# A quarter of the weight split moved from DVE to an accumulating DMA, in a four-mixer encoder layer

## The chip, the cores and the metric

The kernel runs on one core of a Trainium2 chip. The metric is the device time of one execution in microseconds (us). The engines are named as in the profile: PE is TensorE's matmul stream and PEld its weight loads, DVE is VectorE, ACT is ScalarE, POOL is GpSimd, and SP is SyncE, which here only issues DMAs.

## The reference, cut to what matters

One layer of an encoder trunk on 256 tokens of width 2048, all in float32: a norm, a mixer of three kinds of heads, a cross-attention to a memory of 256 tokens, and a convolutional FFN of width 5632. Nearly all of the work is in the products with the seven weight matrices, each used once:

```python
x = _layer_norm(x, ln_in_g, ln_in_b)
for l in range(DEPTH):                       # DEPTH = 1
    mix = _hybrid_mixer(x, w_in[l], ..., w_out[l])
    x = _layer_norm(DN_ALPHA * x + mix, ln1_g[l], ln1_b[l])
    ca = _memory_cross_attention(x, mem, xq[l], xkv[l], xo[l])
    x = _layer_norm(DN_ALPHA * x + ca, ln2_g[l], ln2_b[l])
    ff = _conv_ffn(x, ffn_w_up[l], ffn_conv_w[l], ffn_conv_b[l], ffn_w_down[l])
    x = _layer_norm(DN_ALPHA * x + ff, ln3_g[l], ln3_b[l])
```

## The kernel before

A float32 product is made of three products of the format f32r: each operand is written as a high part plus a low part, and high x high, high x low and low x high are summed in PSUM.

**The weight stream.** The weights lie in HBM in the order of their use and come in tiles of up to 1 MB (128 partitions x 2048 numbers), issued by SP into `wraw`, a pool of three buffers (line 110). `load_w` takes each tile in two halves of up to 128 x 1024. For each half, `split` makes the high part with a cast on ACT (line 142, `hi<-raw`) and the low part with a subtraction on DVE (line 143, `lo<-raw,hi`), into the pool `whl`, which has four buffers for `hi` and four for `lo`. So the split of a half can begin when PE has finished the half four before it, and PE then works on the three halves in between. A `raw` buffer is free for the next load when both its halves are split.

**The products.** `cm_chunk` (lines 155 and 157) computes 256 output channels with the channels on the partitions, `tm_part` (line 178) a token-major product; both walk over the halves in order and after each one call `tick`, which lets the running jobs (attention heads, convolution, norms) put their next few instructions in between.

**The norms.** After each of the first three norms `ln_affine` multiplies the stream `xt` by the norm's gain and adds its bias on POOL, off the main path. It works in four chunks. Each one loads two rows (`gb`, line 264, one buffer), multiplies two tiles (line 275) and adds to two tiles (line 276).

**Order.** Each engine runs its instructions in one fixed order, which a scheduler makes from the program when the kernel is built. An instruction that waits holds up everything behind it on its engine. A DMA is issued from an engine's own queue: when it has to wait for its data, that engine waits.

Of the kernel before, what the change touches and what calls it, by code (L numbers as in the profile page):

```python
# [7 lines left out]
F32 = mybir.dt.float32  # L8
F32R = mybir.dt.float32r
AF = mybir.ActivationFunctionType  # L10
ALU = mybir.AluOpType
AX = mybir.AxisListType

P = 128
D = 2048
S = 256
KT = D // P          # 16 contraction tiles of the model width
NT = S // P          # 2 token tiles
HM = 4               # mLSTM heads
HA = 8               # chunked-attention heads  # L20
HX = 4               # cross-attention heads
DFF = 5632
FT = DFF // P        # 44
CT = 31              # conformer taps
# [3 lines left out]
THREE = ((0, 0), (0, 1), (1, 0))     # the products of high and low parts that float32 sees  # L28
WT = 2048            # elements per partition of one streamed weight tile
WH = WT // 2         # elements per partition of one split weight tile  # L30
COLS = [(0, 512), (512, 1024), (1024, 1536), (1536, 2048)]
COLS_LAST = COLS[:3] + [(1536, 1792), (1792, 2048)]     # before a norm that nothing covers: a short last product
# [3 lines left out]
# per-partition parameter columns  # L36
# [10 lines left out]
def tm_group(n):  # L47
    """contraction tiles in one streamed tile of n token-major columns"""
    return 4 if n > 256 else 8
# [3 lines left out]
def trunk_kernel(ctx: ExitStack, tc: tile.TileContext, plan, x, memT, wts, pvec, rows, gbias, abias, normg, out):  # L53
    nc = tc.nc
    V, A, G = nc.vector, nc.scalar, nc.gpsimd
# [11 lines left out]
    # ---------------------------------------------------------------- constants  # L67
# [12 lines left out]
    def keep_warm(n):  # L80
        """products nobody reads: they hold the tensor engine's clock up where it waits for data"""
        ps = aux.tile([P, 512], F32, name="aux")
        for _ in range(n):
            last = nc.tensor.matmul(ps[:, 0:P], lhsT=ident, rhs=ident, start=True, stop=True)
        return tc.issue_after(last.ins)

    # ---------------------------------------------------------------- weight stream
    woff = [0]
    ready = []
    behind = []  # L90

    def fetch_w(mat, ks, cols):
        """next streamed weight tile: contraction tiles ks of the column ranges; plan records it for the host's layout"""
        n = sum(b - a for a, b in cols)
        sz = len(ks) * n
        raw = wraw.tile([P, WT], F32, name="raw")[:, :sz]
        src = wts[woff[0]:woff[0] + P * sz].rearrange("(p f) -> p f", p=P)
        woff[0] += P * sz
        plan.append((mat, tuple(ks), tuple(cols)))
        return raw, src  # L100

    def load_w(mat, ks, cols):
        """a streamed weight tile in halves, each split into two f32r parts: (contraction tiles, high, low)"""
        hk = step = (len(ks) + 1) // 2
        if ready:
            raw = ready.pop()
            step = 1 if ks[0] == 0 else hk
        else:
            raw, src = fetch_w(mat, ks, cols)
            nc.sync.dma_start(raw, src)  # L110
        n = raw.shape[1] // len(ks)
        for k0 in range(0, len(ks), hk):
            kl = ks[k0:k0 + hk]
            sz = len(kl) * n
            hi = whl.tile([P, WH], F32R, name="hi")[:, :sz]
            lo = whl.tile([P, WH], F32R, name="lo")[:, :sz]
            after = behind.pop(0) if behind else None
            for o in range(0, sz, step * n):
                e = min(o + step * n, sz)
                with tc.issue_after(after) if after else ExitStack():  # L120
                    split(hi[:, o:e], lo[:, o:e], raw[:, k0 * n + o:k0 * n + e])
            yield kl, hi.rearrange("p (k n) -> p k n", n=n), lo.rearrange("p (k n) -> p k n", n=n)

    # work that is spread between the weight tiles: every tick takes each running job one step on
# [11 lines left out]
    def split_to(dst, src):  # L136
        """the two parts of channel tiles [128, tiles, 256] into dst [128, tiles, 2, 256]"""
        split(dst[:, :, 0, :], dst[:, :, 1, :], src)

    def split(hi, lo, src):  # L140
        """src (f32, SBUF or PSUM) = hi + lo, each a f32r number"""
        A.copy(hi, src)  # L142
        V.tensor_sub(lo, src, hi.bitcast(F32))  # L143

    def cm_chunk(a, mat, c0, c1, dst):
        """256 channel-major outputs, 128 from column c0 and 128 from c1: dst[c, j, t] = sum_k W[k, cj + c] a[k, t]

        The two parts of a lie side by side, so that one product takes both of them."""
        ps = mm.tile([P, 2, 2, S], F32, name="mm")
        for g in range(0, KT, 8):  # L150
            for ks, wH, wL in load_w(mat, list(range(g, g + 8)), [(c0, c0 + P), (c1, c1 + P)]):
                for j in range(2):
                    cs = slice(j * P, (j + 1) * P)
                    for kk, k in enumerate(ks):
                        nc.tensor.matmul(ps[:, j], lhsT=wH[:, kk, cs], rhs=a[:, k], start=(k == 0), stop=(k == KT - 1),  # L155
                                         skip_group_check=True)
                        nc.tensor.matmul(ps[:, j, 0, :], lhsT=wL[:, kk, cs], rhs=a[:, k, 0, :], start=False,  # L157
                                         stop=(k == KT - 1), skip_group_check=True)
                tick()
        A.copy(dst, ps[:, :, 1, :])  # L160
        V.tensor_add(dst, dst, ps[:, :, 0, :])
# [5 lines left out]
    def tm_part(ps, a, mat, ks, cols, first=True, last=True, row0=0):  # L167
        """token-major outputs: psum[tt][t, c] += sum_k a[k, t] W[k, c] over the contraction tiles ks"""
# [13 lines left out]
    def tm_by_token(a, mat, ks, cols, row0=0):  # L182
        """as tm_part, one token tile after the other, so that the first one's norm runs under the second one's products"""
# [17 lines left out]
    def act_parts():  # L201
        """both parts of a channel-major operand: [channel, contraction tile, part, token]"""
        return act.tile([P, KT, 2, S], F32R, name="parts")

    # ---------------------------------------------------------------- layer norm
    xt = const.tile([P, NT, D], F32, name="xt")      # residual / pre-norm / normalised stream, in place

    def rsqrt(y, v, n):
        """y = 1/sqrt(v + eps): square root, reciprocal and a Newton step on [128, n]"""
# [10 lines left out]
    def ln_scales(n, tts=range(NT), last=None):  # L220
        """mean and 1 / std of token tiles from n partial statistics"""
# [7 lines left out]
    def ln_normalise(mv, rs, c, tts=range(NT)):  # L229
        """xt <- (xt - mean) / std on a quarter of the channels"""  # L230
# [5 lines left out]
    def ln_transpose(a, gname, bname, k0, nk=2):  # L236
        """channel-major g * z + b of nk channel tiles, split in two parts"""
# [24 lines left out]
    def pool_load(dst, src):  # L262
        """a small load behind what the Pool engine has to do before, off the weights' queue"""
        tc.keep_in_program_order(G.dma_start(dst, src))

    def ln_affine(ri, rs):
        """xt <- g * xt + b along the free dimension, chunk by chunk"""
# [10 lines left out]
    # ---------------------------------------------------------------- start: one head of the memory, input norm  # L278
# [6 lines left out]
    def load_both(mp, g, mat, cols):  # L285
        """a quarter of the memory and its weight tile, in halves that arrive by turns"""
# [48 lines left out]
    # ================================================================ mixer  # L335
    mix = act_parts()
    with tc.tile_pool(name="mx", bufs=1) as mx, tc.tile_pool(name="mx2", bufs=2) as mx2:
        # masks
# [13 lines left out]
        # ---- token-major slices of the projection  # L352
# [5 lines left out]
        # slice 0: gates and the first three value heads  # L358
# [8 lines left out]
        def gate_job():  # L367
            # log sigmoid(f) = min(f, 0) - log1p(e),  e = exp(-|f|),  log1p(e) = e ln(u) / (u - 1),  u = 1 + e
# [17 lines left out]
            # gates as rows: [head, time]  # L386
# [6 lines left out]
            # b = cumsum(log f); a = i - b; mrow = running max of max(a, 0); -m_t = -(b + mrow)  # L393
# [28 lines left out]
        # ---- conformer convolution channels  # L422
# [24 lines left out]
        # layer norm over the 512 channels (partitions x 4): sums by the tensor engine  # L447
# [41 lines left out]
        # ---- chunked attention heads  # L489
# [44 lines left out]
        # ---- mLSTM heads  # L534
# [5 lines left out]
        def mlstm_job(h, qp):  # L540
# [7 lines left out]
            # decay weights exp(a_s - mrow_t), keys on the partitions  # L548
# [29 lines left out]
        # normaliser max(|den|, exp(-m_t)), head norm and output gate  # L578
# [44 lines left out]
        # ---- output projection: the mLSTM channels come last  # L623
# [6 lines left out]
    # ---------------------------------------------------------------- residual + statistics of a token-major product  # L630
# [22 lines left out]
    # ================================================================ memory cross-attention  # L653
# [94 lines left out]
    # ================================================================ convolutional FFN  # L748
# [30 lines left out]
    # ---------------------------------------------------------------- output norm  # L779
# [73 lines left out]
```

## Time and profile before

| | |
|---|---|
| three runs | 1549.06, 1550.57, 1554.81 us; median 1550.57 |
| span of the profiled execution | 1549.5 us, first to last instruction |
| PE, DVE, ACT, POOL busy | 1522.2, 1022.2, 758.8, 141.3 us |
| DMA | 292.87 MB, of which the weights' queue 282.64 MB |
| weight halves on PE | 536 splits, each a cast on ACT and a subtraction on DVE |

The page gives the profiled execution by its span only, which lies 1.1 us under the median of the three runs. Busy shares are of the span. A wait counts only where the engine that waits is the one whose end sets the time.

### The profile page before, as it was taken

What the parts mean: (1) busy time and instruction counts of PE and PEld (TensorE: products, weight loads), DVE (VectorE), ACT (ScalarE), POOL (GpSimd) and SP (SyncE); (2) the same over time, 40 slices, a digit from 0 to 9 for tenths busy, and PEclk for the clock granted to TensorE, in tenths of its full rate; (3) what the DMA queues carried; (4) which work ended last, traced back from release to release, by engine and by line L of the source; (5) the groups of instructions that cost most, each with busy time, mean ns of one, the idle gap of its engine ahead of it and who ended that gap; (6) DMA issues with size and microseconds to landing.
All of it is one profiled execution on the core that took longest, in us unless ns stands there. A gap on an engine that the chain in (4) does not pass through costs nothing.

```text
span 1549.5 us, 20637 instructions
## 1 busy us (share of the span) xinstructions
PE 1522.2 (98%) x8218; PEld 1314.6 (85%) x8218; DVE 1022.2 (66%) x1346; ACT 758.8 (49%) x986; POOL 141.3 (9%) x138
## 2 busy tenths in 40 slices
PE   8999999999999999999989999999999999999995
PEld 7988888888888888888878888888888888888885
DVE  6765999678776545665579665566656665556666
ACT  5554454676454445454355554454534554455542
POOL 0350000100006300000036000000000000000002
PEclk9999999999999999999999999999999999999998
DMA  9565545444656654444555555545555554655452
GB/s 344 177 231 191 190 173 179 168 170 160 236 202 216 218 192 170 157 140 159 192 202 204 202 187 183 199 183 188 177 204 190 191 191 170 209 192 184 175 177 90
DMA packets 46127, 292.87 MB, mean 189 GB/s; under 512 B 5392, under 2 KB 6032, under 8 KB 15312
## 3 DMA queue, kind: packets, MB, share of 16 engines
q1 hardware_dynamic: 43056, 282.64, 50.3%
q0 software_dynamic: 2544, 8.13, 2.3%
q8 instruction: 64, 1.05, 0.3%
q10 hardware_dynamic: 432, 0.79, 0.1%
q14 instruction: 31, 0.25, 0.0%
HBM read 289.44 MB, written 2.10 MB: 188 GB/s over the span
## 4 chain that ended last, share of the span: by engine, by line
PE 97%; DVE 1%; DMA 0%; POOL 0%; ACT 0%; POOLq 0%; issue 0%; SPq 0%; ACTq 0%
PE mm L178 37%; PE mm L155 37%; PE mm L157 19%; PE mm L192 1%; PE aux L681 1%; PE aux L711 1%; PE aux L242 1%; DMA mraw<-memT_in 0%; DVE xt L797 0%; PE aux L500 0%; PE aux L521 0%; POOL parts L247 0%; PE aux L516 0%; PE aux L550 0%; DVE xt L798 0%; PE aux L499 0%
## 5 line engine op out<-in xcount | busy, mean ns | idle before, releaser
L143 DVE TENSOR_TENSOR lo<-raw,hi 128x1024 fp32r<-128x1024 f32 (+4 forms) x536 | 657.3, 1230 | 446.8 <-ACT hi L142 442.0
L155 PE MATMUL mm<-parts,hi 128*128 128x512 f32 x2432 | 864.9, 400 | 3.3 <-POOL parts L247 3.0
L142 ACT CAST hi<-raw 128x1024 fp32r<-128x1024 f32 (+4 forms) x536 | 548.4, 1025 | 640.3 <-PE mm L155 320.7
L157 PE MATMUL mm<-parts,lo 128*128 128x256 f32 x2432 | 684.2, 281 | 0.0
L155 PEld LDWEIGHTS mm<-parts,hi 128*128 128x128 f32 x2432 | 457.6, 188 | 115.4 <-POOL parts L247 3.5
L157 PEld LDWEIGHTS mm<-parts,lo 128*128 128x128 f32 x2432 | 460.4, 189 | 0.5
L178 PE MATMUL mm<-hi,parts 128*128 128x512 f32 (+3 forms) x1088 | 316.9, 373 | 2.1 <-ACT hi L142 2.1
L178 PEld LDWEIGHTS mm<-hi,parts 128*128 128x128 f32 x1088 | 200.6, 189 | 35.0 <-ACT hi L142 2.3
L178 PE MATMUL mm<-hi,hp 128*128 128x512 f32 (+1 forms) x704 | 211.9, 383 | 0.0
L178 PE MATMUL mm<-lo,parts 128*128 128x512 f32 (+3 forms) x544 | 202.8, 373 | 0.2 <-DVE lo L143 0.2
L178 PEld LDWEIGHTS mm<-hi,hp 128*128 128x128 f32 x704 | 130.9, 188 | 25.8
L178 PE MATMUL mm<-lo,hp 128*128 128x512 f32 (+1 forms) x352 | 134.7, 383 | 0.0
L178 PEld LDWEIGHTS mm<-lo,parts 128*128 128x128 f32 x544 | 102.9, 189 | 16.4 <-DVE lo L143 0.5
L178 PEld LDWEIGHTS mm<-lo,hp 128*128 128x128 f32 x352 | 66.2, 188 | 12.7
L794 POOL TENSOR_TENSOR xt<-xt,gb 128x512 f32<-128x512 f32 x3 | 4.5, 1498 | 685.8 <-ACT xt L793 685.8
L247 POOL TENSOR_TENSOR parts<-y,parts 128x512 fp32r<-128x512 f32 (+1 forms) x12 | 18.5, 1539 | 454.0 <-DVE parts L246 454.0
L439 DVE SCALAR_TENSOR_TENSOR cac<-cpad,pv,cac 128x256 f32<-128x256 f32 x120 | 51.2, 481 | 0.0
L766 DVE SCALAR_TENSOR_TENSOR ac<-gv,pv,ac 128x255 f32<-128x255 f32 x88 | 50.1, 569 | 1.6
L142 ACT CAST hp<-ac 128x256 fp32r<-128x256 f32 x44 | 17.9, 406 | 56.3 <-DVE ac L768 56.3
L275 POOL TENSOR_TENSOR xt<-xt,gb 128x512 f32<-128x512 f32 x24 | 41.1, 1732 | 45.7 <-DMA gb<-rows_in 34.9
L276 POOL TENSOR_TENSOR xt<-xt,gb 128x512 f32<-128x512 f32 x24 | 42.1, 1775 | 0.7 <-DMA gb<-rows_in 0.7
L143 DVE TENSOR_TENSOR hp<-ac,hp 128x256 fp32r<-128x256 f32 x44 | 18.7, 426 | 20.3 <-ACT hp L142 20.3
(227 smaller groups left out, 758.8 us busy)
## 6 DMA issues: line engine op xcount, KB each, us to landing
raw<-wts_in SPq DMA_DIRECT2D x238, 1024.0 KB, 4.8
raw<-wts_in SPq DMA_DIRECT2D x19, 768.0 KB, 4.3
gb<-rows_in POOLq DMA_DIRECT2D x24, 256.0 KB, 5.5
raw<-wts_in SPq DMA_DIRECT2D x4, 784.0 KB, 4.3
raw<-wts_in SPq DMA_DIRECT2D x6, 512.0 KB, 7.8
xt<-x_in SPq DMA_DIRECT2D x4, 512.0 KB, 10.4
raw<-memT_in SPq DMA_DIRECT2D x4, 512.0 KB, 3.1
gb<-rows_in SPq DMA_DIRECT2D x2, 1024.0 KB, 5.6
```

The source lines that it names most:

```text
L142: A.copy(hi, src)
L143: V.tensor_sub(lo, src, hi.bitcast(F32))
L155: nc.tensor.matmul(ps[:, j], lhsT=wH[:, kk, cs], rhs=a[:, k], start=(k == 0), stop=(k == KT - 1), skip_group_check=True)
L157: nc.tensor.matmul(ps[:, j, 0, :], lhsT=wL[:, kk, cs], rhs=a[:, k, 0, :], start=False, stop=(k == KT - 1), skip_group_check=True)
L178: nc.tensor.matmul(ps[tt][:, :n], lhsT=a[:, k, part, tsl], rhs=w[:, kk, :], start=(first and k == ks[0] and i == 0), stop=(last and k == k ...
L192: nc.tensor.matmul(ps[tt][:, :n], lhsT=a[:, k, part, tt * P:(tt + 1) * P], rhs=w[:, kk, :], start=(k == ks[0] and i == 0), stop=(k == ks[- ...
L242: nc.tensor.transpose(ps[:, k, tt * P:(tt + 1) * P], xt[:, tt, (k0 + k) * P:(k0 + k + 1) * P], ident)
L247: (G if k0 % 4 == 2 else V).tensor_sub(lo, y[:, 0:nk, :], hi.bitcast(F32))
L275: G.tensor_mul(sl, sl, gb[:, 0, :])
L276: G.tensor_add(sl, sl, gb[:, 1, :])
L439: tap = V.scalar_tensor_tensor(cac[:, i, :], cpad[:, i, j:j + S], pcol("ccw", i * CT + j), cac[:, i, :], ALU.mult, ALU.add)
L766: V.scalar_tensor_tensor(ac[:, o:], gv[:, 0, 0:S - o], pcol("fcw", f * 3 + t), ac[:, o:], ALU.mult, ALU.add)
```

## The change

Every fourth split (a counter `nsplit` over the splits, skipping those at the very start that come in quarter tiles and those held behind another instruction) makes its low part in another way: ACT casts the high part as before, ACT then writes the negated high part into `lo`, and a DMA issued by POOL adds `raw` onto it. By the program this happens 132 times: 118 of 128x1024, the others smaller.

```diff
@@ load_w @@
                 with tc.issue_after(after) if after else ExitStack():
-                    split(hi[:, o:e], lo[:, o:e], raw[:, k0 * n + o:k0 * n + e])
+                    nsplit[0] += 1
+                    if step == hk and not after and nsplit[0] % 4 == 0:
+                        split_by_dma(hi[:, o:e], lo[:, o:e], raw[:, k0 * n + o:k0 * n + e])
+                    else:
+                        split(hi[:, o:e], lo[:, o:e], raw[:, k0 * n + o:k0 * n + e])
...
     def split(hi, lo, src):
         A.copy(hi, src)
         V.tensor_sub(lo, src, hi.bitcast(F32))
 
+    def split_by_dma(hi, lo, src):
+        A.copy(hi, src)
+        A.mul(lo, hi.bitcast(F32), -1.0)
+        G.dma_start(lo.bitcast(F32), src, accum_op=ALU.add)
```

In the changed program the lines are some eleven further down: the casts of the changed halves are line 152, the negations 153, the accumulating DMAs 154; `ln_affine` stands at 275 to 287 and the other splits at 147 and 148.

POOL, at the norm after the mixer, before: the four chunks of `ln_affine` stand behind the four `parts` subtractions, and nothing else is in between.

```order
L247 TENSOR_TENSOR parts<-y,parts 128x2x256 x4
L268 COPY begun<-rs 128x2
L264 DMA gb<-rows_in 128x512 x2
L275 TENSOR_TENSOR xt<-xt,gb 128x512 x2
L276 TENSOR_TENSOR xt<-xt,gb 128x512 x2
L264 DMA gb<-rows_in 128x512 x2
L275 TENSOR_TENSOR xt<-xt,gb 128x512 x2
L276 TENSOR_TENSOR xt<-xt,gb 128x512 x2
```

The same place after the change, from the last accumulating DMA (`lo<-raw`) ahead of the norm's chunks to the second chunk's end and on.

```order
L154 DMA lo<-raw 128x1024
L258 TENSOR_TENSOR parts<-y,parts 128x2x256
L279 COPY begun<-rs 128x2
L275 DMA gb<-rows_in 128x512 x2
L286 TENSOR_TENSOR xt<-xt,gb 128x512 x2
L287 TENSOR_TENSOR xt<-xt,gb 128x512 x2
L275 DMA gb<-rows_in 128x512 x2
L286 TENSOR_TENSOR xt<-xt,gb 128x512 x2
L287 TENSOR_TENSOR xt<-xt,gb 128x512 x2
L154 DMA lo<-raw 128x1024
L275 DMA gb<-rows_in 128x512 x2
L286 TENSOR_TENSOR xt<-xt,gb 128x512 x2
```

Between two consecutive accumulating DMAs POOL has two whole chunks here, and two more before the third. At the norm behind the input two chunks stand between the second and the third DMA of the stretch and nearly two before the next; at the norm after the cross-attention three chunks stand between two DMAs, and one before the next.

ACT, in the FFN's `up` products, after the change: `hi` are the casts, `gv`, `ac` and `hp` the FFN's own tiles.

```order
L147 CAST hi<-raw 128x1024 x2
L171 COPY gv<-mm 128x512
L147 CAST hi<-raw 128x1024
L774 ACTIVATE ac<-gv,pv 128x256
L152 CAST hi<-raw 128x1024
L778 ACTIVATE ac<-ac 128x256
L153 ACTIVATE lo<-hi 128x1024
L147 CAST hp<-ac 128x256
```

The negation has come in behind the FFN's activation, ahead of the cast of `hp`; one half in four has it. The order of the products on PE is the same but for a few instructions of the jobs.

## Rows read from the trace of the kernel before

**Rows 1.** The page's busy time of each engine, share of the span, instructions.
```profile
PE 1522.2 (98%) x8218; PEld 1314.6 (85%) x8218; DVE 1022.2 (66%) x1346; ACT 758.8 (49%) x986; POOL 141.3 (9%) x138
```
**Rows 2.** Waits of PE: in total (us), how often, longest.
```profile
PE mm L155 <- POOL parts L247: 3.0, 1, 3.0
...
PE mm L178 <- DVE lo L143: 0.2, 1, 0.2
```
**Rows 3.** The two groups of the split: busy us, mean ns, idle before.
```profile
L143 DVE TENSOR_TENSOR lo<-raw,hi 128x1024 fp32r<-128x1024 f32 (+4 forms) x536 | 657.3, 1230 | 446.8 <-ACT hi L142 442.0
...
L142 ACT CAST hi<-raw 128x1024 fp32r<-128x1024 f32 (+4 forms) x536 | 548.4, 1025 | 640.3 <-PE mm L155 320.7
```
**Rows 4.** Timeline of ACT in the FFN: start us, us, instruction, idle before.
```profile
863.33 1.05 ACT L142 CAST hi<-raw 128x1024 fp32r<-128x1024 f32 x1 [1.61 <-PE mm L155]
...
866.17 1.05 ACT L142 CAST hi<-raw 128x1024 fp32r<-128x1024 f32 x1 [1.30 <-PE mm L155]
...
868.99 1.05 ACT L142 CAST hi<-raw 128x1024 fp32r<-128x1024 f32 x1 [1.27 <-PE mm L155]
869.94 0.41 ACT L767 ACTIVATE ac<-ac 128x256 f32<-128x256 f32 x1
```
**Rows 5.** DMA issues: queue, count, KB each, us from issue to landing.
```profile
raw<-wts_in SPq DMA_DIRECT2D x238, 1024.0 KB, 4.8
...
gb<-rows_in POOLq DMA_DIRECT2D x24, 256.0 KB, 5.5
...
raw<-wts_in SPq DMA_DIRECT2D x6, 512.0 KB, 7.8
...
raw<-memT_in SPq DMA_DIRECT2D x4, 512.0 KB, 3.1
```
**Rows 6.** Timeline of POOL at the three norms of the stream.
```profile
89.33 1.11 POOL L264 DMA_DIRECT2D gb<-rows_in  x2 [0.30 <-POOL xt L276]
...
110.08 4.52 POOL L276 TENSOR_TENSOR xt<-xt,gb 128x512 f32<-128x512 f32 x2
...
492.72 4.51 POOL L276 TENSOR_TENSOR xt<-xt,gb 128x512 f32<-128x512 f32 x2
...
517.55 3.52 POOL L276 TENSOR_TENSOR xt<-xt,gb 128x512 f32<-128x512 f32 x2
...
835.93 2.90 POOL L276 TENSOR_TENSOR xt<-xt,gb 128x512 f32<-128x512 f32 x2
...
847.71 2.90 POOL L276 TENSOR_TENSOR xt<-xt,gb 128x512 f32<-128x512 f32 x2
```
**Rows 7.** Timeline of ACT: casts that PE released at the same three norms.
```profile
77.38 0.84 ACT L142 CAST hi<-raw 128x768 fp32r<-128x768 f32 x1 [0.98 <-ACT gm L361]
...
89.36 1.05 ACT L142 CAST hi<-raw 128x1024 fp32r<-128x1024 f32 x1 [1.23 <-PE mm L178]
...
482.62 1.05 ACT L142 CAST hi<-raw 128x1024 fp32r<-128x1024 f32 x1 [1.24 <-PE mm L155]
...
493.71 1.06 ACT L142 CAST hi<-raw 128x1024 fp32r<-128x1024 f32 x1 [1.24 <-PE mm L155]
...
820.93 1.05 ACT L142 CAST hi<-raw 128x1024 fp32r<-128x1024 f32 x1 [1.29 <-PE mm L155]
```
**Rows 8.** The start: ACT's cast of the sixth half.
```profile
19.45 1.06 ACT L142 CAST hi<-raw 128x1024 fp32r<-128x1024 f32 x1 [0.38 <-DMA raw<-wts_in]
```
**Rows 9.** The start: instructions on `lo` by stage; PE's are products, four a half.
```profile
8.50:23.90 15.40, 8.69 (x20) 4.29 (x21) 7.24 (x9) 0.89 1.03 399
```
**Rows 10.** POOL behind a bias load of an attention head.
```profile
223.48 0.14 POOL L528 MEMSET bt<- 64x64 f32 x1 [2.09 <-DMA bt<-abias_in]
```
**Rows 11.** ACT at the end of an FFN block's `down` columns: a half of half size.
```profile
1109.67 0.62 ACT L142 CAST hi<-raw 128x512 fp32r<-128x512 f32 x1 [1.17 <-PE mm L178]
```
**Rows 12.** Busy time by stage after PE waited 3.0 us; third last column: granted clock.
```profile
793.80:797.10 3.30, 3.30 (x13) 2.91 (x13) 2.31 (x5) 2.32 (x6) 1.28 (x1) 0.50 0.66 273
```

More of the change, by code (lines that the diff above doesn't have):

```diff
@@ L88, in trunk_kernel @@
     woff = [0]
+    nsplit = [0]
     ready = []
```

## The prediction, made before the changed kernel ran

> **What bounds the kernel now.** I read the page's busy shares first, then who PE waits for, then the timeline around one split. PE is busy for 98% of the span [rows 1], and its waits are few: the longest on POOL is 3.0 us, and it waited for a low part once, for 0.2 us [rows 2]. So the time is PE's, and a change elsewhere can gain nearly nothing; it costs as soon as a `lo` is late. DVE's 536 subtractions of 1.23 us and ACT's casts of 1.03 us are off the path; ACT's idle time ahead of a cast ends mostly on PE [rows 3], since the cast waits for the buffer of the half four before. That gives the pace: casts in the FFN start 2.83 us apart, each when PE ends a half [rows 4]. From the start of a cast, PE has three halves to work through before it needs the result: 3 x 2.83 = **8.5 us of lead**. Cast plus subtraction take 2.3 us of it.
>
> **What the change removes.** 132 subtractions on DVE, some 132 x 1.23 = 162 us of busy time. PE waits for them for 0.2 us in all, so I count this at zero.
>
> **What it adds on ACT.** 132 negations. No row has one; the cast reads and writes as many numbers, so I take 1.05 us: 139 us, which lifts ACT from 49% to 58%. ACT idles over a microsecond ahead of most casts [rows 4], which hides it; without that cover, it would cost at most those 139 us.
>
> **What it adds per changed half: a DMA.** The trace has no accumulating DMA. It must read `raw` and `lo` and write `lo`, 512 KB each. Call X the time from its issue to the landing. The lower bound is a plain load of 512 KB, 3.1 us; the upper the same size at the start, when the rings are full, 7.8 us [rows 5]. The nearest rows are the load that reads as many bytes as this one (1 MB, 4.8 us) and POOL's own row loads (5.5 us) [rows 5], so I take **X = 5.2 us**. The Trainium skill, page "DMA: Bandwidth & Descriptors", section "Anatomy of one DMA", gives about 2.0 us plus bytes / 436 GB/s for a DMA from this queue, an estimated 3.2 us for a copy of 512 KB. The Trainium skill's page "Collectives: The Full Stack", section "The bandwidth ceiling", says that an add in the DMA engine costs its second source read and not the adding; with the bytes doubled the estimate is 4.4 us. No row here shows either; by 3.2 us the time would come out near 1643 us, by 4.4 us near 1656.
>
> In the steady state a changed half then takes cast 1.05, activation in between 0.41 [rows 4], negation 1.05, a hand-over of about 0.1 (my estimate) and X = 5.2: 7.8 us of the 8.5. **Zero**, but with 0.7 us to spare: past X of about 5.9 in the FFN, and 6.3 elsewhere, each further microsecond costs one on nearly every changed half, some 100 us in all (118 are of full size; I leave out those with a longer lead).
>
> The `raw` buffer is held 5.5 us longer (7.8 against 2.3). Its next content is first cast five halves, 14.2 us, after this half's cast, and the load takes 4.8 us, so 1.6 us remain: zero, and with it gone the cost is again a microsecond for a microsecond.
>
> **What it moves: POOL's queue.** The DMA waits on POOL for the negation, and stands behind whatever POOL does. Changed halves come every four halves, 11.3 us. After PE has begun one, the next is due 11.3 later, so POOL must issue it within 11.3 - 5.2 = 6.1 us, 1.1 us after its negation is done. At the three norms the order puts two or three chunks of `ln_affine` between two DMAs, and a chunk takes some 11.9 us (two of them end at 497.2 and the next two at 521.1 [rows 6]), since it waits for its row loads. I take POOL's times from the trace and count a half's start on PE as the cast three halves later, which PE's end of the half ahead releases.
>
> - Input norm. PE reaches the half at 77.4 [rows 7]. POOL issues it after the third chunk's row loads, at 89.33 + 1.11, plus 0.55 for the other DMA that now stands ahead: 91.0 [rows 6]. This half has 768 columns, X = 4.6 (estimate). Landed at 95.6: **18.2 us**. The next is due 12.0 later [rows 7], at 107.6; POOL ends the fourth chunk at 114.6 [rows 6], issues two DMAs, landed 120.3: **12.7**.
> - After the mixer: due 482.6 [rows 7]; the second chunk ends at 497.2 [rows 6]; landed 502.4: **19.8**. Next due 11.1 later, 513.5; the fourth chunk ends at 521.1, plus 0.55, landed 526.8: **13.3**.
> - After the cross-attention: due 820.9 [rows 7]; third chunk ends at 838.8 [rows 6], plus 0.55, landed 844.6: **23.7**. Next due 855.9; fourth chunk ends at 850.6 plus 1.1, landed 856.9: **1.0**.
>
> Together **88.7 us**. What could hide it is PE's lead alone, and that is in the reckoning.
>
> **Smaller terms.** At the start the first changed half is the sixth. Its cast is at 19.45 [rows 8]; PE reaches it at 23.9, after twenty low products, five halves [rows 9]. Cast, a cast of the memory of 0.6, negation: 22.2; with the start's 7.8 us it lands at 30.0: **6.1**. Each of eight attention heads holds POOL 2.1 us for a bias load plus its issue [rows 10], in front of one changed half; I take 0.5 each, **4** (bounds 0 and 2.7 each, 22). At the end of each FFN block's columns a half has half the size [rows 11], so the lead there is 1.4 us shorter, at most 7.1 against 7.4 (no activation in between); two a block, four blocks, I take 0.6 each since token-major halves look a little shorter: **5**. And the clock: after PE's wait of 3.0 us it ran 3.3 us at 0.50 of full speed, 1.2 GHz [rows 2, 12], which loses 1.7 us. Six waits above are longer than 3 us: **10**.
>
> **Sum.** 88.7 + 6.1 + 4 + 5 + 10 = 114 us onto the span of 1549.5, so 1663.5; the median of the runs shown is 1.1 above the span, so the time is **1665 us**, 7% slower.
>
> **The rivals.**
> *The accumulating DMA is slow.* The add may run at less than half the copying rate, or meet the weight loads, which are just then due. For it: POOL's 256 KB loads take 5.5 us where SP's 512 KB take 3.1 [rows 5]. Against: the 1 MB load needs only 1.7 us more than the 512 KB one. With X = 7.0, about 1.0 over the spare on 100 halves is 100 us, and 1.8 on seven placed waits 13: near 1780 us. With X = 7.8 near 1865.
> *The norms' blocks don't hold.* If the loads of rows came at once and POOL's operations ran at the pace of the single issue, the DMAs would go out within the lead. It decides when two chunks take under some 12 us; they take 24 now, and a pair of additions alone 2.9 to 4.5 [rows 6]. Then the 88.7 us and most of the clock's loss go: 1567 us.
> *DVE's relief pays, not slower.* With 162 us less on DVE, what waits for DVE in the joints at the norms would come earlier. It decides if no changed half is late: X under 4 us and POOL free at each. PE is idle for only 1549.5 - 1522.2 = 27 us in all [rows 1], most of it start and tail, so the price is at most some 5 us: 1545 to 1551. The order of POOL speaks against it.
>
> **How the numbers follow.** Forecast 0.63, slow DMA 0.28, blocks that don't hold 0.06, relief 0.03. The forecast's own range is 1632 to 1700: at X = 3.1 the six waits at POOL and the two small terms fall by 13 + 9, and without the clock's loss by 10 more, 1633; at X = 6.2 a few waits open. The range of 8 in 10 starts there and reaches into the slow DMA up to X of about 7.7, 1850 us; beyond it I leave 0.1, below it 0.09. Half a per cent is about what a measurement of this kernel can tell. Faster 0.01, same 0.02, slower 0.97, since each case but the last is slower.
>
> **What would show it.** In the changed profile POOL's DMAs (line 154) should land 5 us after issue; PE's waits should name a DMA `lo<-raw` with some six long ones, 10 to 24 us, at the three norms and one at the start, and hardly any in the FFN's steady stretches; the granted clock should dip after each. The prediction fails if PE waits in most FFN blocks (X too small), or if the waits at the norms are under 5 us each (POOL faster, or the lead longer than I count).

## The result, and the profile after

The changed kernel takes 1658.28 us (median of 4 runs, 1654.06 to 1660.6), the kernel before 1550.43 us on the same chip (1549.06 to 1554.81): a ratio of 1.068, with a 95% interval of 1.067 to 1.070. It is slower by 108 us; 1665 was forecast. The figures of the runs below leave out one execution of the changed kernel with copies, which took 2548 us at a mean granted clock of 0.555 where the other three took 1634 to 1638.

The page of the changed kernel: span, busy time of each engine, and the two DMA queues that carry the weights (q1) and POOL's transfers (q0), with their packets, MB and share of 16 engines' time.

```profile
span 1652.3 us, 21108 instructions
...
PE 1540.6 (93%) x8218; PEld 1325.8 (80%) x8218; DVE 860.5 (52%) x1214; ACT 885.3 (54%) x1118; POOL 246.6 (15%) x270
...
q1 hardware_dynamic: 43056, 282.64, 45.0%
q0 software_dynamic: 21552, 73.96, 23.2%
```

Against [rows 1]: DVE lost 162 us of work and ACT gained 127, as the edit says. PE has as many instructions as before, is busy 18.4 us longer (1540.6 against 1522.2) and idle 84.4 us longer (111.7 against 27.3). The two make the whole difference of the spans, 102.8 us. Who PE waited for (total us, times, longest):

```profile
PE mm L168 <- DMA lo<-raw: 51.2, 7, 18.3
PE mm L189 <- DMA lo<-raw: 32.9, 6, 11.8
PE mm L166 <- POOL parts L258: 3.0, 1, 3.0
...
PE mm L189 <- DVE lo L148: 1.0, 2, 0.8
```

The first two rows are new: 84.1 us in 13 waits on the accumulating DMA. The wait on POOL of [rows 2] stands as it was, and the one on DVE stays small, 1.0 us where it was 0.2. The same view cut to stretches of the span shows where (start; input norm; heads in two rows; after the mixer; after the cross-attention; the FFN and the output norm):

```profile
PE mm L189 <- DMA lo<-raw: 6.2, 1, 6.2
PE mm L168 <- DMA lo<-raw: 1.8, 1, 1.8
...
PE mm L189 <- DMA lo<-raw: 23.2, 3, 11.8
...
PE mm L189 <- DMA lo<-raw: 3.4, 2, 1.8
PE mm L168 <- DMA lo<-raw: 2.7, 1, 2.7
...
PE mm L168 <- DMA lo<-raw: 26.3, 2, 18.3
...
PE mm L168 <- DMA lo<-raw: 20.2, 2, 18.3
...
PE mm L168 <- DMA lo<-raw: 0.3, 1, 0.3
```

So 69.7 of the 84.1 us fall at the three norms, 8.0 at the start, 6.1 in the heads, and 0.3 in the whole FFN, where 64 of the 132 DMAs run. The groups that answer to [rows 3], and the DMA issues that answer to [rows 5]:

```profile
L154 POOL DMA_DIRECT2D lo<-raw x132 | 114.1, 864 | 1229.3 <-ACT lo L153 781.2
...
L153 ACT ACTIVATE lo<-hi 128x1024 fp32r<-128x1024 f32 (+3 forms) x132 | 133.7, 1013 | 2.5
```
```profile
raw<-wts_in SPq DMA_DIRECT2D x238, 1024.0 KB, 5.5
lo<-raw POOLq DMA_DIRECT2D x118, 512.0 KB, 4.5
```

An accumulating DMA of 512 KB lands 4.5 us after its issue in the median (X in the prediction), and the issue holds POOL for 0.86 us. The weight loads now take 5.5 us instead of 4.8. From the end of ACT's negation to POOL's issue 0.29 us pass in the median and at most 1.6 us in 127 of the 132; in the other five, all at the norms, it is 9.6 to 19.5 us, and PE's waits for these five make 64.7 of the 84.1 us. What happens at a norm is seen best on POOL's timeline behind the mixer, where the chunks of `ln_affine` are:

```profile
532.13 1.11 POOL L275 DMA_DIRECT2D gb<-rows_in  x2 [0.30 <-POOL xt L287]
536.38 2.48 POOL L286 TENSOR_TENSOR xt<-xt,gb 128x512 f32<-128x512 f32 x2 [3.13 <-DMA gb<-rows_in]
538.82 2.48 POOL L287 TENSOR_TENSOR xt<-xt,gb 128x512 f32<-128x512 f32 x2
541.24 0.89 POOL L154 DMA_DIRECT2D lo<-raw  x1
...
549.63 2.52 POOL L287 TENSOR_TENSOR xt<-xt,gb 128x512 f32<-128x512 f32 x2
...
559.15 4.45 POOL L287 TENSOR_TENSOR xt<-xt,gb 128x512 f32<-128x512 f32 x2
563.54 0.90 POOL L154 DMA_DIRECT2D lo<-raw  x1
```

The issue at 541.24 follows the second chunk's arithmetic without a gap, and the one at 563.54 the fourth chunk's. ACT's negation for the first of them, and PE's first product with its low part:

```profile
520.68 1.06 ACT L153 ACTIVATE lo<-hi 128x1024 fp32r<-128x1024 f32 x1
...
546.45 0.58 PE L168 MATMUL mm<-parts,lo 128*128 128x256 f32 x1 [18.28 <-DMA lo<-raw]
```

ACT was done at 521.74, 19.5 us ahead of the issue. What held the issue back was the chunks that stand ahead of it in POOL's order, their arithmetic and their wait for the row loads. The clock then (start and end, length, busy us of PE, PEld, DVE, ACT and POOL; the third last column is the granted clock):

```profile
530.80:551.30 20.50, 4.85 (x16) 4.17 (x17) 0.00 (x0) 0.00 (x0) 13.16 (x14) 0.50 0.53 139
```

Around this wait PE has the lower of its two clock levels, 1.2 GHz, and keeps it for the first 4.8 us of work behind the wait. Just there (another stretch of the same view)

```profile
547.10:552.20 5.10, 5.10 (x19) 4.31 (x19) 0.00 (x0) 0.81 (x1) 5.00 (x4) 0.59 0.90 344
```

19 matmuls kept PE busy for 5.1 us, 0.27 us each; in the kernel before, with the same kinds of products behind the mixer's norm, it was

```profile
490.40:497.30 6.90, 6.90 (x41) 6.06 (x40) 4.89 (x4) 3.41 (x4) 6.83 (x4) 1.00 0.63 237
```

41 in 6.9, 0.17 us each, at the full clock. The lower level stands around the other long waits too, and that is how PE's busy time grew; how much of the 18.4 us it makes is reckoned below.

### The profile page after: what moved, and what is told of

Its sections match the earlier page's. It is cut to its first block, busy times and chain, and to the rows that moved or that the text cites. A ratio compares the mean times of both kernels' runs of the same rounds, so it can differ in the third digit from the quotient of the medians.

```text
span 1652.3 us, 21108 instructions
## 1 busy us (share of the span) xinstructions
PE 1540.6 (93%) x8218; PEld 1325.8 (80%) x8218; DVE 860.5 (52%) x1214; ACT 885.3 (54%) x1118; POOL 246.6 (15%) x270
## 3 DMA queue, kind: packets, MB, share of 16 engines
q1 hardware_dynamic: 43056, 282.64, 45.0%
q0 software_dynamic: 21552, 73.96, 23.2%
## 4 chain that ended last, share of the span: by engine, by line
PE 59%; DMA 3%; POOL 1%; ACT 1%; DVE 1%; issue 0%; POOLq 0%; ACTq 0%; DVEq 0%
PE mm L166 23%; PE mm L189 20%; PE mm L168 12%; DMA lo<-raw 2%; PE mm L203 1%; DMA gb<-rows_in 1%; PE aux L692 1%; PE aux L722 1%; POOL xt L287 1%; POOL xt L286 0%; ACT lo L153 0%; ACT hi L152 0%; POOL parts L258 0%; DVE xt L808 0%; PE aux L253 0%
## 5 line engine op out<-in xcount | busy, mean ns | idle before, releaser
L148 DVE TENSOR_TENSOR lo<-raw,hi 128x1024 fp32r<-128x1024 f32 (+2 forms) x404 | 491.2, 1218 | 558.2 <-ACT hi L147 557.3
L147 ACT CAST hi<-raw 128x1024 fp32r<-128x1024 f32 (+2 forms) x404 | 416.2, 1031 | 424.5 <-PE mm L166 239.2
L189 PE MATMUL mm<-hi,parts 128*128 128x512 f32 (+3 forms) x1088 | 321.5, 377 | 0.6 <-ACT hi L147 0.6
L154 POOL DMA_DIRECT2D lo<-raw x132 | 114.1, 864 | 1229.3 <-ACT lo L153 781.2
L152 ACT CAST hi<-raw 128x1024 fp32r<-128x1024 f32 (+3 forms) x132 | 133.0, 1007 | 253.9 <-PE mm L166 146.2
L189 PE MATMUL mm<-lo,parts 128*128 128x512 f32 (+3 forms) x544 | 206.2, 379 | 33.9 <-DMA lo<-raw 32.9
L189 PEld LDWEIGHTS mm<-hi,parts 128*128 128x128 f32 x1088 | 204.3, 192 | 33.9 <-ACT hi L147 1.3
L153 ACT ACTIVATE lo<-hi 128x1024 fp32r<-128x1024 f32 (+3 forms) x132 | 133.7, 1013 | 2.5
L779 DVE TENSOR_TENSOR ac<-gv,ac 128x256 f32<-128x256 f32 x44 | 18.9, 429 | 62.9 <-ACT ac L778 62.9
L777 DVE SCALAR_TENSOR_TENSOR ac<-gv,pv,ac 128x255 f32<-128x255 f32 x88 | 45.2, 514 | 1.6
L286 POOL TENSOR_TENSOR xt<-xt,gb 128x512 f32<-128x512 f32 x24 | 35.0, 1476 | 42.4 <-DMA gb<-rows_in 42.4
L287 POOL TENSOR_TENSOR xt<-xt,gb 128x512 f32<-128x512 f32 x24 | 40.9, 1724 | 0.1
```

The source lines that it names most:

```text
L153: A.mul(lo, hi.bitcast(F32), -1.0)
L154: G.dma_start(lo.bitcast(F32), src, accum_op=ALU.add)
L189: nc.tensor.matmul(ps[tt][:, :n], lhsT=a[:, k, part, tsl], rhs=w[:, kk, :], start=(first and k == ks[0] and i == 0), stop=(last and k == k ...
L286: G.tensor_mul(sl, sl, gb[:, 0, :])
L287: G.tensor_add(sl, sl, gb[:, 1, :])
L777: V.scalar_tensor_tensor(ac[:, o:], gv[:, 0, 0:S - o], pcol("fcw", f * 3 + t), ac[:, o:], ALU.mult, ALU.add)
```

## Experiments

**The norms spared.** The twelve halves whose DMA falls into a norm's stretch go back to DVE; the other 120 keep the DMA.

```
-   if step == hk and not after and nsplit[0] % 4 == 0:
+   if step == hk and not after and nsplit[0] % 4 == 0 and nsplit[0] not in (
+           28, 32, 36, 40, 44, 164, 168, 172, 176, 272, 276, 280):
```

> The changed kernel, but the twelve changed halves that fall due while POOL works on a norm's four chunks are split on DVE again; 120 accumulating DMAs stay. Theory (the loss is POOL's queue: a DMA stands behind the chunks): the five waits of 12.2, 8.6, 18.5, 8.2 and 18.6 us go, 66 us, and with them most of the slow clock, 12 us: near 1580 us (1570 to 1590), and PE's waits on an accumulating DMA fall from 84 us to about 18. Rival (every accumulating DMA costs a little, 108 us over 132 of them, 0.8 each): twelve fewer save 10 us, 1648 us.

Measured: 1580.55 us, ratio 1.019 (1.0175 to 1.0205). PE's waits on the DMA fell from 84.1 to 17.7 us:

```profile
PE mm L189 <- DMA lo<-raw: 11.6, 4, 4.6
PE mm L168 <- DMA lo<-raw: 5.6, 5, 2.7
```

Twelve of 132 DMAs carry 78 of the 108 us. A price on every DMA is out.

**The negation without the DMA.** DVE adds the raw weights to the negated high part, so that ACT's new work stays and POOL's goes.

```
-        G.dma_start(lo.bitcast(F32), src, accum_op=ALU.add)
+        V.tensor_add(lo, lo.bitcast(F32), src)
```

> The changed kernel, but the negated high part is completed by an addition on DVE and not by a DMA: ACT's 132 extra passes stay, POOL and the DMA rings are as before. Theory (ACT's passes are hidden): 1551 us within 0.3%, no wait of PE above 3 us. Rival (ACT's 134 us, which stand ahead of evictions and the FFN's casts, cost part of the loss): 1560 us or more.

Measured: 1557.9 us, ratio 1.0035 (1.0023 to 1.0047), between the two. So 127 us more work on ACT cost some 5 us, not nothing. The trace has 2.3 us of it in one new wait, the second row: ACT had cast this half by 314.96 and negated it by 316.86, and DVE, busy with other work, began the addition at 318.79. The wait of the first row is 3.0 us in the kernel before.

```profile
PE aux L400 <- DVE gm L395: 3.5, 1, 3.5
...
PE mm L168 <- DVE lo L154: 2.3, 1, 2.3
```

**The DMA in the FFN alone** (halves after the 280th), 64 DMAs, 54 of them of full size.

```
-   if step == hk and not after and nsplit[0] % 4 == 0:
+   if step == hk and not after and nsplit[0] % 4 == 0 and nsplit[0] > 280:
```

> The changed kernel with accumulating DMAs only in the FFN, behind the last norm's chunks; 64 of the 132 stay. Theory (a DMA of 4.5 us fits in the lead of 8.5, and POOL is free there): 1552 us (1549 to 1555). Rival (0.8 us for each): 1600 us.

Measured: 1555.9 us, ratio 1.0026 (1.0013 to 1.0039); 4 us over the kernel before, and 0.9 above the 1549 to 1555 that were expected. The trace shows 2.5 us of it as three waits for the DMA. So in the FFN the DMA is hidden but for little, and 0.8 us for each is out.

**Every second half of the FFN**, 128 DMAs, to see how much spare there is.

```
-   if step == hk and not after and nsplit[0] % 4 == 0:
+   if step == hk and not after and nsplit[0] % 2 == 0 and nsplit[0] > 280:
```

> As the run with accumulating DMAs in the FFN only, but for every second half there, so that twice as many run. In the FFN the rings are 53% busy before and about 75% in the changed kernel, so about 97% here. Theory (only a late low part costs, and X may grow from 4.5 to 5.9 us before that): 1552 to 1575 us, with PE's waits on the DMA or on weight loads in the FFN. Rival (0.8 us for each): 1650 us.

Measured: 1701.74 us, ratio 1.094 (1.0895 to 1.0993). Both theories missed. The waits are many, none over 9.2 us, and X is 5.7 us in the median:

```profile
PE mm L168 <- DMA lo<-raw: 72.1, 34, 9.2
PE mm L189 <- DMA lo<-raw: 29.3, 19, 3.8
```

Three runs looked for the cause. The first replaced the source, so that the raw buffer is free early:

```
+   if step == hk and not after and nsplit[0] % 2 == 0 and nsplit[0] > 280:
...
-        G.dma_start(lo.bitcast(F32), src, accum_op=ALU.add)
+        G.dma_start(lo.bitcast(F32), k0.rearrange("p a s -> p (a s)")[:, :lo.shape[1]], accum_op=ALU.add)
```

> As in the run with every second half tile of the FFN by DMA (1702 us), but the DMA adds a resident tile that is idle in the FFN (k0), not the raw weights, so that the raw buffer is free as soon as ACT has read it. The low parts then hold other numbers. Theory A (the loss came from the raw buffer, held some 5 us longer by the DMA, so that the next weight load starts late): the waits of ACT on the weight loads go and the time falls back to 1553 to 1590. Theory B (the loss came from the two kinds of transfer meeting on the 16 DMA engines): X stays at 5.5 us and above, and the time stays above 1670.

Measured: 1673.86 us, ratio 1.080 (1.0758 to 1.0839), with X at a median of 6.3 us. Holding the raw buffer explains some 28 us (1701.74 less 1673.86) of some 150, if the other source changes nothing else. Theory A is out, and theory B came true in both numbers, the time only just, which does not yet show its reason.

**A copy in place of the add**, first in the changed kernel. The subtraction is left out: the low part is the whole weight.

```
-        G.dma_start(lo.bitcast(F32), src, accum_op=ALU.add)
+        G.dma_start(lo.bitcast(F32), src)
```

> The same 132 DMAs from the same places, but each copies the raw weights over the negated high part in place of adding to it (the subtraction is left out, the low part is the whole weight). It prices the add inside X, which is 4.5 us for 512 KB. Theory (the add makes the transfer read its destination too, so bytes moved are what X is made of): X falls to 3 to 3.7 us, POOL's ring takes a third less of the DMA engines' time, each of some 16 waits is about 1 us shorter, and the time is 1630 to 1650. Rival (X is a fixed cost of the issue from POOL and of completion): X stays at 4.2 to 4.6 and the time at 1653 to 1662.

Measured: 1634.3 us (median of three), ratio 1.055 (1.0529 to 1.0565), as the theory has it. The order of every engine's instructions is that of the changed kernel. The row of POOL's queue and the issue's row:

```profile
q0 software_dynamic: 20592, 73.96, 12.2%
...
lo<-raw POOLq DMA_DIRECT2D x118, 512.0 KB, 2.9
```

The add is 1.6 us of the 4.5, and almost half of what the queue takes of the engines' time (23.2% against 12.2%; a third was expected). The Trainium skill's page "DMA: Bandwidth & Descriptors", section "Anatomy of one DMA", puts a copy of 512 KB at an estimated 3.2 us. The Trainium skill's page "Collectives: The Full Stack", section "The bandwidth ceiling", says of the reduce step of a collective that its add costs a second source read; with the bytes doubled for it the estimate is 4.4. The runs come near both, with 2.9 and 4.5.

**Copies at every second half of the FFN** (both edits above; the same part is left out).

> As the run with every second half tile of the FFN by DMA (1702 us), but each DMA copies the raw weights over the negated high part in place of adding (the low part is then the whole weight). The raw buffer is held for the same reason, the issues are the same. Theory (the 16 DMA engines run out: their share in the FFN is 0.53 without these DMAs, 0.74 with an add at every fourth half, 0.62 with a copy at every fourth half, so 0.95 is wanted with adds at every second half and 0.71 with copies): with copies the share is 0.68 to 0.74, X is 3 to 3.5 us, and the time is 1550 to 1570. Rival (the issues follow each other too closely on POOL's queue, or the raw buffer is held too long, whatever the bytes): waits on the low part stay above 40 us and the time above 1620.

Measured: 1598.26 us, ratio 1.032 (1.0273 to 1.0357), between the two, with X at a median of 4.4 us, where 3 to 3.5 was expected. The stretch from 1000 to 1200 us of six kernels, last columns clock, share of the DMA engines' time and GB/s; before:

```profile
1000.00:1200.00 200.00, 200.00 (x1059) 171.19 (x1058) 119.93 (x143) 95.72 (x123) 0.00 (x0) 1.00 0.53 189
```
adds at every fourth half (the changed kernel), copies at every fourth:
```profile
1000.00:1200.00 200.00, 199.90 (x1055) 170.13 (x1054) 99.73 (x125) 112.43 (x142) 15.48 (x18) 1.00 0.74 235
```
```profile
1000.00:1200.00 200.00, 200.00 (x1039) 170.42 (x1038) 99.88 (x124) 112.18 (x141) 9.55 (x18) 1.00 0.62 234
```
adds from the raw weights and from the resident tile at every second half, and copies at every second:
```profile
1000.00:1200.00 200.00, 174.01 (x874) 145.75 (x873) 66.02 (x91) 107.37 (x134) 26.12 (x30) 0.95 0.84 227
```
```profile
1000.00:1200.00 200.00, 181.30 (x918) 151.18 (x919) 67.47 (x92) 113.14 (x139) 26.98 (x31) 0.97 0.90 242
```
```profile
1000.00:1200.00 200.00, 190.92 (x991) 161.20 (x990) 73.81 (x98) 122.25 (x148) 18.19 (x35) 0.99 0.74 265
```

Copies took two thirds of the loss away (some 150 to 47 us over the kernel before). They ask less of the DMA engines (POOL's queue has 12.3% of their time, with adds 22.0%), but a copy alone also lands 1.6 us sooner and holds POOL for 0.53 us and not 0.86; this run does not tell these apart. The average share is not the whole reason in any case: at the same share of 0.74, adds at every fourth half cost PE 0.1 us of these 200, copies at every second 9.1. One thing that differs is how often the two kinds of transfer meet. From the issue and landing times between 950 and 1550 us I counted the DMAs that had a weight load in flight from 1 to 2 us after their issue: 12 of 55 in the changed kernel, 76 of 104 with copies at every second half. In the latter those 76 have a median X of 5.1 us, the other 28 of 2.9. In the changed kernel, though, the 12 have 4.7 and the others 4.5. That meetings make X longer is what the copies argue and the adds at every fourth half hardly show; no run changed the meeting alone, and why every second half costs so much stays open.

**The norm's arithmetic spread**, all 132 DMAs kept. `ln_affine` is made a job that takes one step a tick (after the input norm it starts with the mixer's jobs), with four ticks between a chunk's row loads and its arithmetic and four behind it; the added DMA and the arithmetic keep their written order on POOL.

```
-        ln_affine(ri, rs)
+        if ri == 0:
+            late.append(ln_affine(ri, rs))
+        else:
+            yield from ln_affine(ri, rs)
...
+            for _ in range(4):
+                yield
             for tt in range(NT):
                 sl = xt[:, tt, c * 512:(c + 1) * 512]
-                G.tensor_mul(sl, sl, gb[:, 0, :])
-                G.tensor_add(sl, sl, gb[:, 1, :])
+                tc.keep_in_program_order(G.tensor_mul(sl, sl, gb[:, 0, :]))
+                tc.keep_in_program_order(G.tensor_add(sl, sl, gb[:, 1, :]))
+            for _ in range(4):
+                yield
...
-    ln_affine(4, rs)
+    jobs.append(ln_affine(4, rs))
...
-        G.dma_start(lo.bitcast(F32), src, accum_op=ALU.add)
+        tc.keep_in_program_order(G.dma_start(lo.bitcast(F32), src, accum_op=ALU.add))
```

> All 132 low parts still come from the DMA. Only the norm's arithmetic on POOL is handed out over the weight tiles, so that between two accumulating DMAs POOL has one row load's issue or one chunk's four operations (about 7 us) and no more. Theory (the waits at the three norms are the DMA's issue standing behind POOL's own queue): the waits there shrink from about 72 us to below 15, and the time comes down towards that of the kernel that spares the norms, 1580 us; taken range 1575 to 1605. Rival (the accumulating DMA is slow at a norm because it meets the row loads on the DMA engines, or because PE's clock is low there anyway): X is above 6 us at the norms even with a short queue, and the time stays at 1630 to 1660.

Measured: 1634.41 us, ratio 1.054 (1.0526 to 1.0561): the rival's band. But the waits at the norms did shrink, to 17.1 us (3.6, 4.3 and 9.2), a little over the 15 that were expected, with X at the norms at 5.2 in the median and over 6 in two of 21. The waits had moved to the heads, where they rose from 6.1 to 19.7 us, since the fixed order put the DMA behind a bias load (ACT had negated this half by 264.39; POOL's order had the load first, which waited for PE), on POOL's timeline:

```profile
275.97 0.56 POOL L279 DMA_DIRECT2D bt<-abias_in  x1 [15.91 <-PE aux L536]
280.19 0.14 POOL L548 MEMSET bt<- 64x64 f32 x1 [3.65 <-DMA bt<-abias_in]
...
280.68 0.86 POOL L155 DMA_DIRECT2D lo<-raw  x1 [0.26 <-issue]
```

So this run alone does not decide between the two. The next run frees the heads: the order is fixed near the norms alone, and the last norm's arithmetic starts four ticks later.

```
-        tc.keep_in_program_order(G.dma_start(lo.bitcast(F32), src, accum_op=ALU.add))
+        d = G.dma_start(lo.bitcast(F32), src, accum_op=ALU.add)
+        if nsplit[0] < 80 or 160 < nsplit[0] < 200 or 264 < nsplit[0] < 320:
+            tc.keep_in_program_order(d)
```

> As the run that spreads the norm's arithmetic (1634 us), but a DMA is fixed to its place in POOL's program order near the three norms alone; in the heads between them it may go ahead of the bias loads and memsets as in the changed kernel, and the arithmetic at the last norm begins four ticks later. The run before had some 20 us of waits at the norms (72 in the changed kernel) and lost some 40 us in the attention heads, where three DMAs stood 8 to 17 us behind a bias load. Theory (what is paid at a norm and in those heads is one thing, the issue standing behind other work in POOL's queue): the heads cost what they cost in the changed kernel and the time is 1583 to 1605. Rival (the spread arithmetic or its row loads disturb the heads by themselves): 1615 to 1640.

Measured: 1596.93 us, ratio 1.030 (1.0277 to 1.0328), inside the theory's range. PE's waits on the DMA are 27.7 us in all; in the stretches of the three norms they are

```profile
PE mm L192 <- DMA lo<-raw: 2.0, 1, 2.0
...
PE mm L171 <- DMA lo<-raw: 8.6, 1, 8.6
...
PE mm L171 <- DMA lo<-raw: 3.5, 5, 1.5
```

With the same 132 DMAs and the same arithmetic, the three norms now cost 14.1 us of waits where the changed kernel has 69.7. Only the order on POOL differs: PE, DVE, ACT and SP run the same instructions in the same order as in the changed kernel, one for one. So some 60 us of the 108 are shown to be POOL's order by itself. I saw no version that would beat the kernel before, since PE is busy for 98% of its span.

## Why the prediction was right

The mechanism was the forecast's, and so was each of its places but the heads. By its own terms, forecast and then measured (waits of PE by stretch; the clock by PE's added busy time), in us:

| term | forecast | measured |
|---|---|---|
| three norms | 88.7 | 69.7 (23.2, 26.3, 20.2) |
| start | 6.1 | 8.0 |
| heads | 4 | 6.1 |
| FFN's short halves | 5 | 0.3 |
| clock | 10 | 18.4 |
| sum | 114 | 102.5, of 102.8 on the span |

*DVE's relief at zero: right.* 162 us of DVE work gone show nowhere in the time. The rival in which relief pays is out with the sign. In the run with the DMA in the FFN alone DVE has 62 us less to do than in the kernel before (960.3 against 1022.2), and the time is 4 us longer.

*ACT's negations at zero: nearly right.* Without the DMA the negation costs some 5 us (1557.9). The cover of idle time that I named holds in steady state. It fails in the heads, once in that run, and in the changed kernel in the waits told of under the heads below. I did not measure what of these 5 us remains when the DMA's longer waits stand in front of it.

*X: too large by 0.7 us in the median, not where it counted.* Forecast 5.2 from the nearest rows [rows 5], measured 4.5, made of 2.9 for a copy and 1.6 for the add. But by their issue and landing times the DMAs of the three longest waits took 6.3, 5.2 and 5.2 us, where I had 4.6, 5.2 and 5.2. Two more, issued at the input norm and behind the cross-attention right after the first row loads, took 6.3 and 6.9 us and brought waits of 3.2 and 1.8 us that I had not placed. The rival of a slow DMA needed X at 7 throughout; the median came near that only with twice as many in the FFN (6.3).

*Steady state at zero: right, and closer to the edge than it looks.* Every fourth half costs 0.3 us of waits in the whole FFN (2.5 in the run with the FFN alone), every second half some 150 us of time. The 0.7 us to spare that I reckoned was 1.4: from the cast to the landing 7.1 us pass in the FFN's median. But X itself does not stay at 4.5 when the DMAs come more often. That X depends on how many there are was not in my reckoning; here it did no harm.

*POOL's queue at the norms: right in kind, 19 us too much.* The runs that spare the norms and that spread their arithmetic both take the waits away, the second without taking any DMA away. For the three longest waits 18.2, 19.8 and 23.7 us were forecast and 11.8, 18.3 and 18.3 measured. Counted in us from the start of POOL's copy `begun`, which opens a norm's chunks, in the kernel before (from which I reckoned, with PE's coming read as in the prediction) and in the changed one:

| norm | PE comes to the half: before, changed | POOL is free to issue: before, changed |
|---|---|---|
| input | 13.6, 18.5 | 26.7, 24.1 |
| after the mixer | 11.8, 12.7 | 26.4, 25.8 |
| after the cross-attention | 16.5, 21.1 | 34.4, 34.3 |

So I had POOL's pace nearly right; it was free 0.1 to 2.6 us sooner. PE came about 1 to 4.9 us later, which makes 10.5 of the 13.2 us by which these three waits fell short. At the input norm and behind the cross-attention it had just waited the 3.2 and 1.8 us that I had not placed, and it had run at the lower clock behind them. The second wait behind the mixer shrank in the same way, from 13.3 to 8.0: PE came to that half 13.7 us after the end of the first wait, where 11.1 was reckoned at the full clock.

*The clock: too small by 8 us.* I priced six waits at the 1.7 us that the one wait of 3.0 us cost [rows 2, 12]. The price nearly holds (PE works 3.0 to 6.2 us in each stretch of the lower level, and half of that is lost), the number does not: leaving out the tail, in which PE does nothing, the lower level stands in ten stretches of the changed kernel, around waits of 1.8 to 3.2 us too, and in two of the kernel before. Summed over the ten and over the two:

```profile
sum 92.20, PE 40.76 PEld 36.96 DVE 12.49 ACT 7.92 POOL 43.67; mean PE 4.08 PEld 3.70 DVE 1.25 ACT 0.79 POOL 4.37
...
sum 6.90, PE 6.88 PEld 5.72 DVE 4.85 ACT 4.45 POOL 1.99; mean PE 3.44 PEld 2.86 DVE 2.43 ACT 2.23 POOL 0.99
```

PE works 33.9 us longer at half the clock; half of that, an estimated 17 us, is nearly all of the 18.4. What the clock takes from PE ahead of a half that is late anyway, it takes off that half's wait, so this error and part of the norms' are two sides of one. That the rest nearly cancels is luck, and the sum is closer than its terms.

*Start: right in place.* The start's DMA took 8.19 us, where 7.8 was taken, and a second one, of 7.76 us, was late by 1.8.

*Heads: near in size by luck.* I had the DMA held on POOL by bias loads. The 6.1 us are three waits, and POOL stood idle ahead of each of their issues, until ACT had negated:

```profile
350.57 0.86 POOL L154 DMA_DIRECT2D lo<-raw  x1 [11.24 <-ACT lo L153]
...
394.36 0.86 POOL L154 DMA_DIRECT2D lo<-raw  x1 [15.62 <-ACT lo L153]
...
441.73 0.86 POOL L154 DMA_DIRECT2D lo<-raw  x1 [12.85 <-ACT lo L153]
```

In the first two other work of ACT stood between the cast and the negation (cast at 346.47 and 389.26, negation at 349.21 and 393.00); in the third the cast ahead of this half's had waited 2.52 us for a weight load. So the 4.5 us of the first two go with the negation, which I had put at zero, and not with the bias loads.

## What to carry to other kernels

A transfer that replaces an engine's operation has to be priced where it is issued: a queue that is idle on average (POOL, 9% busy) can still hold an issue back for twenty microseconds where its own work comes in blocks, and an in-order queue passes that on to whoever needs the data. List what stands ahead of each new instruction on its queue, place by place, and compare it with the consumer's lead there; the steady state says little about the joints. When an order is fixed by hand to mend one place, look at the other places where the same queue waits for something.

## What the runs showed of the hardware

A pair of POOL's additions on 128x512 f32 took 2.48 us at 538.82 above. DVE did nothing then, for 24.56 us ahead of this subtraction:

```profile
555.27 1.23 DVE L148 TENSOR_TENSOR lo<-raw,hi 128x1024 fp32r<-128x1024 f32 x1 [24.56 <-ACT hi L147]
```

Such a pair took 4.51 in the kernel before [rows 6], where DVE was busy for 4.89 of 6.9 us (the stretch from 490.4). The Trainium skill's page "SBUF — State Buffer", section "Who interferes with whom", says that a DVE operation with two SBUF inputs contends with a POOL operation that reads SBUF, for a port pair that is locked and not shared; the rows agree, without showing the lock itself.

An accumulating DMA within SBUF took 4.5 us for 512 KB in the median and a copy 2.9; three of 384 to 512 KB that were issued right behind a norm's row loads took 6.3 to 6.9. The issue held POOL for 0.86 us against 0.53 for the copy. With 132 adds POOL's queue (73.96 MB) took 23.2% of the 16 engines' time, half of what the loads took for 282.64 MB.
